# Second MLP product of a decoder block: from feature-major to token-major, each quarter as Strassen's seven half products

## The chip, the cores and the metric

The kernel runs on one core of a Trainium2 chip. The metric is the device time of one execution in microseconds (us); lower is better. Three timed runs of the kernel before gave 912.48, 912.89 and 913.3 us.

Engine names in all views: PE is the tensor engine (matmul), PEld its weight load, DVE the vector engine, ACT the scalar engine, SP the engine whose queue issues every DMA of this kernel.

## What is computed

One residual block over 512 tokens of width 1024, all in float32. The part that changes is the last one, a squared-ReLU MLP of inner width 4096:

```python
h2 = rms_norm(x) * (1.0 + scale2) + shift2
ff = jnp.square(jax.nn.relu(h2 @ w_ff1[l])) @ w_ff2[l]
x = x + gate2 * ff
```

Everything ahead of it (modulation, one input projection, a recurrent branch, a differential attention branch, their gated merge) stays as it was.

## The kernel before, in words

A float32 product runs as three passes of a faster format, float32r: every operand is split into H (rounded, by an ACT copy) and L (the rest, by a DVE subtraction), and `mm3` (L123 to L126) issues H\*H, H\*L and L\*H. Each pass is one matmul of a 128x128 stationary operand and 512 moving columns. Activations lie feature-major, 128 features by 512 tokens in a chunk, and the weights are stationary.

`load_w` brings a weight block of 128x1024 (512 KB) by DMA into one of three `w` buffers and splits it into `wh` (ACT, L118) and `wl` (DVE, L119), two buffers of each. `project` (L128) then runs 8 chunks times 3 passes = 24 matmuls into one PSUM bank.

The MLP goes in four quarters of the inner width (`qd` 0 to 3). In the first half of a quarter, the hidden half, 8 blocks of `w_ff1` are projected; each result gets ReLU (ACT, L828), is squared (DVE, L829) and split into `rh` (ACT, L833) and `rlo` (DVE, L138). In the second half 8 blocks of `w_ff2` are projected from these chunks, and DVE adds each result times gate2 into `x1` (L854). In quarter 0 two hidden blocks (`f1e`) run early, before the norm is known, and eight chunks of the modulation (`ada_chunk`, L183 on DVE, from a `w` buffer too) are computed beside the second product. The last block of all runs in two halves of the tokens (L847), each with its own output DMA.

The order of instructions on each engine is fixed when the program is built: a scheduler orders them by priority (`tc.high_priority(HP)` moves the weight splits ahead of other work), and each engine then takes its own in that order, waiting on semaphores where an operand or a buffer is not ready.

Of the kernel before, what the change touches and what calls it, by code (L numbers as in the profile page):

```python
# [44 lines left out]
DV0, DV1 = (0,), (0,)      # token blocks that the vector engine scales  # L45
# [3 lines left out]
# columns of the per-feature parameter table  # L49
# [4 lines left out]
def build(tc, out, x, xT_in, c, pos, vecs, reps, ada, w_xr, w_xr7, w_qk, w_v, w_gr, w_gm, w_lru,  # L54
# [4 lines left out]
    with ExitStack() as es:  # L59
# [21 lines left out]
        def rsqrt(dst, src, n, mul, eps, name):  # L81
            """dst = 1/sqrt(src*mul + eps), [P, n] float32, Newton from a bit-pattern seed."""
# [40 lines left out]
        def mm3(ps, lh, ll, rh, rl, first, last):  # L123
            nc.tensor.matmul(ps, lh, rh, start=first, stop=False)  # L124
            nc.tensor.matmul(ps, lh, rl, start=False, stop=False)  # L125
            nc.tensor.matmul(ps, ll, rh, start=False, stop=last)  # L126
# [35 lines left out]
        # silu(c) on every partition  # L162
# [23 lines left out]
        def ada_halves(j, k, prev=None):  # L186
            """The same in two halves of the width, from other buffers than the weights'."""
# [27 lines left out]
        # keeps the tensor engine's clock up until the first products; not read  # L215
# [17 lines left out]
        def bcast_cols(src, name, *where):  # L233
            """[P tokens, 4] -> PSUM [P, 512] with the token values on every partition."""
# [8 lines left out]
        def scale_x(j, cols, dve, p_act=None):  # L243
            """x * rs of a part of the width: blocks dve on the vector engine."""
# [14 lines left out]
        NK = 7      # blocks of the first projection that accumulate chunk by chunk  # L259
# [33 lines left out]
        rep = tmp.tile([P, 6, 64], F32, name="rep", tag="a", bufs=B_A)  # L293
# [31 lines left out]
        # sp4 = 4*softplus(-lam) = 8*s*(1 + p) + 4*max(-lam, 0)  # L325
# [14 lines left out]
        nlam = const.tile([P, 1], F32, name="nlam")   # -lambda  # L340
# [5 lines left out]
        # rope angles [P tokens, 4 blocks, 32]  # L346
# [106 lines left out]
        def lru_scan(n, a, u, prev):  # L453
            # a = exp(-8 r sp), sqrt(1 - a^2) = sqrt(tanh(4 r sp)) * (1 + a)
# [49 lines left out]
        def qk_quarter(qt):  # L504
            """q and k of two heads, token-major: rms norm, rope."""
# [28 lines left out]
        def qk_transpose(qt, rot):  # L534
            """to [2 maps x 64, tokens] (H, L), per head (q, k)"""
# [15 lines left out]
        def softmax_step(hd, q, k, i, rr):  # L551
            """e0 - lam * (s0 / s1) * e1 for one query block; 1/s0, 1/s1 go to rr."""
# [6 lines left out]
            # the two maps hold different rows of the array  # L559
# [39 lines left out]
        def head_norm(hd, po, rr):  # L599
            # o = po * r0; y = o / rms(o): one factor r0 * rsqrt(mean(po^2) r0^2 + eps)  # L600
# [18 lines left out]
        def head_out(hd, o1):  # L619
            """y^T [v features, tokens] (H, L)"""  # L620
# [46 lines left out]
        def fill():  # L667
            """The products beside the attention heads, in the order of PLAN."""
# [70 lines left out]
        # sigmoid(z) = (1 + tanh(z/2)) / 2; the halves go into gate1  # L739
# [17 lines left out]
        for n in range(KC):  # L757
# [12 lines left out]
            # x1 * (1 + scale2), before the norm  # L770
# [5 lines left out]
        shf = const.tile([P, 8, 2], F32R, name="shf")      # shift2 as (H, L)  # L776
# [10 lines left out]
        rb2 = t_("rb2s", tag="a")  # L787
# [31 lines left out]
        for qd in range(4):  # L819
            r2_ = []  # L820
            for n in range(KC):
                rl = t_(f"rl{qd}_{n}")
# [6 lines left out]
                nc.vector.tensor_tensor(rl, rl, rl, op=ALU.mult)  # L829
                i = 2 * n  # L830
                tags = [("y", B_Y)] * 2 if qd % 2 == 1 else [("q", B_Q) if i + j < 12 else ("v", B_V) for j in (0, 1)]
                rh = slot(*tags[0], f"rh{qd}_{n}", F32R)
                nc.scalar.copy(rh, rl)  # L833
                rlo = slot(*tags[1], f"rlo{qd}_{n}", F32R)
                split_l(rlo, rl, rh)
                r2_.append((rh, rlo))
            for n in range(KC):
                if qd == 3 and n == KC - 1:
                    # the last block in two halves of the tokens: a short tail
                    wh, wl = load_w(w_ff2[qd, n])  # L840
                    for hf in range(2):
                        cols = slice(hf * 256, hf * 256 + 256)
                        ps = bank(f"f2_{qd}_{n}_{hf}")[:, :256]
                        for k in range(KC):
                            c0 = slice(k * P, (k + 1) * P)
                            mm3(ps, wh[:, c0], wl[:, c0], r2_[k][0][:, cols], r2_[k][1][:, cols], k == 0, k == KC - 1)
# [76 lines left out]
```

## Time and profile before

| what | value |
|---|---|
| timed runs | 912.48, 912.89, 913.3 us |
| profiled execution, span from first to last instruction | 910.9 us |
| what lies around the span (median of the runs less the span; the page names no total of its own) | 2.0 us |
| PE, DVE, ACT busy in the span | 899.2, 572.2, 388.7 us |
| first matmul of the first second product (quarter 0) | at 602.36 us |
| one half of a quarter (192 matmuls) | 43.5 us |
| last matmul starts | at 907.46 us |

The views read are: the page (busy time by engine, granted clock in 40 slices), busy time by stretch, groups of instructions by line, and the timeline, in which a row gives start and duration in us, engine, line, operation, output<-inputs, and in brackets the idle time before it with what ended it. A PE row's duration is modelled and overlaps the next row; the distance between starts is what a matmul costs.

### The profile page before, as it was taken

Reading aid. Unit: us, or ns where it says so; the run is one execution under the profiler, and the core shown is the slowest. Engines: PE = TensorE matmul, PEld = TensorE weight load, DVE = VectorE, ACT = ScalarE, POOL = GpSimd, SP = SyncE. Lnnn points to the kernel's source line nnn. Section 1 sums busy time; section 2 is a strip of 40 time slices with the busy share of each in tenths; the row PEclk is TensorE's granted clock in tenths of the full one; section 3 lists DMA queues with packets and bytes.
Section 4 is the critical chain, followed back from the end, with each engine's and each line's share of the span. In section 5 each row is a group of like instructions: output and inputs, shape, how many; then the busy total and the mean of one; then the engine's idle time right before and its main releaser. Section 6 shows DMA issues by size and latency. Waiting matters only on the chain.

```text
span 910.9 us, 11122 instructions
## 1 busy us (share of the span) xinstructions
PE 899.2 (99%) x4204; PEld 723.0 (79%) x4204; DVE 572.2 (63%) x1080; ACT 388.7 (43%) x676; POOL 2.1 (0%) x40
## 2 busy tenths in 40 slices
PE   6999999999999999999999999999999999999998
PEld 3888887777867878777788888888888888888887
DVE  6963975697879755997758556866343344434442
ACT  6663648964454433445433333531232233213420
POOL 0000000000000000000000000000000000000000
PEclk9999999999999999999999999999999999999999
DMA  9843222122211432444445332255233222332231
GB/s 324 334 152 103 93 92 70 47 70 70 92 63 55 140 114 98 157 150 141 140 146 199 119 121 73 93 183 187 94 106 102 93 92 93 101 108 93 92 139 47
DMA packets 34473, 108.98 MB, mean 120 GB/s; under 512 B 4082, under 2 KB 4466, under 8 KB 34420
## 3 DMA queue, kind: packets, MB, share of 16 engines
q1 hardware_dynamic: 34420, 108.28, 35.0%
q8 instruction: 33, 0.54, 0.2%
q14 instruction: 20, 0.16, 0.1%
HBM read 106.17 MB, written 2.10 MB: 119 GB/s over the span
## 4 chain that ended last, share of the span: by engine, by line
PE 91%; DVE 5%; DMA 2%; ACT 1%; issue 1%; SPq 0%; ACTq 0%; DVEq 0%
PE f L124 12%; PE f L125 12%; PE f L126 12%; PE gm L125 3%; PE gm L124 3%; PE gm L126 3%; PE sc L563 3%; PE qk L126 2%; PE qk L124 2%; PE qk L125 2%; PE po L596 2%; PE v L124 2%; PE v L126 2%; PE v L125 2%; PE xr L126 2%; PE xr L124 2%
## 5 line engine op out<-in xcount | busy, mean ns | idle before, releaser
L118 ACT CAST wh<-w 128x1024 fp32r<-128x1024 f32 (+1 forms) x145 | 151.7, 1046 | 353.5 <-PE f L125 177.1
L119 DVE TENSOR_TENSOR wl<-w,wh 128x1024 fp32r<-128x1024 f32 (+1 forms) x145 | 176.3, 1216 | 124.4 <-ACT wh L118 119.8
L125 PE MATMUL f<-rlo,wh 128*128 128x512 f32 (+1 forms) x264 | 101.1, 383 | 0.0
L126 PE MATMUL f<-rh,wl 128*128 128x512 f32 (+1 forms) x264 | 101.0, 383 | 0.0
L124 PE MATMUL f<-rh,wh 128*128 128x512 f32 (+1 forms) x264 | 101.0, 383 | 0.0
L126 PE MATMUL f<-h2h,wl 128*128 128x512 f32 x240 | 93.3, 390 | 0.1
L124 PE MATMUL f<-h2h,wh 128*128 128x512 f32 x240 | 93.2, 390 | 0.0
L125 PE MATMUL f<-h2l,wh 128*128 128x512 f32 x240 | 92.7, 389 | 0.0
L854 DVE SCALAR_TENSOR_TENSOR x<-f,mod,x 128x512 f32<-128x512 f32 x31 | 23.3, 751 | 87.4 <-PE f L126 87.4
L125 PEld LDWEIGHTS f<-rlo,wh 128*128 128x128 f32 x264 | 49.6, 188 | 10.0 <-DVE rlo L138 0.4
L126 PEld LDWEIGHTS f<-rh,wl 128*128 128x128 f32 x264 | 49.6, 188 | 9.7
L124 PEld LDWEIGHTS f<-rh,wh 128*128 128x128 f32 x264 | 49.6, 188 | 9.7
L126 PEld LDWEIGHTS f<-h2h,wl 128*128 128x128 f32 x240 | 45.0, 188 | 10.0 <-DVE wl L119 0.6
L125 PEld LDWEIGHTS f<-h2l,wh 128*128 128x128 f32 x240 | 45.1, 188 | 9.4
L124 PEld LDWEIGHTS f<-h2h,wh 128*128 128x128 f32 x240 | 45.0, 188 | 9.2
L183 DVE CUSTOM_DVE_ANT_0 ada<-ada,cb,bada 128x1024 f32<-128x1024 f32 x32 | 41.0, 1282 | 17.2 <-DMA ada<-in_ada 17.1
L124 PE MATMUL gm<-hh,wh 128*128 128x512 f32 x128 | 51.5, 402 | 0.0
L126 PE MATMUL gm<-hh,wl 128*128 128x512 f32 x128 | 51.5, 402 | 0.0
L124 PE MATMUL qk<-wh,hh 128*128 128x512 f32 x128 | 51.2, 400 | 0.0
L125 PE MATMUL gm<-hl,wh 128*128 128x512 f32 x128 | 51.1, 399 | 0.0
L126 PE MATMUL qk<-wh,hl 128*128 128x512 f32 x128 | 50.7, 396 | 0.0
L125 PE MATMUL qk<-wl,hh 128*128 128x512 f32 x128 | 50.4, 393 | 0.0
(317 smaller groups left out, 1752.1 us busy)
## 6 DMA issues: line engine op xcount, KB each, us to landing
w<-in_w_ff SPq DMA_DIRECT2D x64, 512.0 KB, 3.2
ada<-in_ada SPq DMA_DIRECT2D x32, 512.0 KB, 3.3
ada<-in_ada SPq DMA_DIRECT2D x32, 256.0 KB, 5.8
w<-in_w_qk SPq DMA_DIRECT2D x16, 512.0 KB, 3.2
w<-in_w_gm SPq DMA_DIRECT2D x16, 512.0 KB, 3.3
w<-in_w_gr SPq DMA_DIRECT2D x8, 512.0 KB, 3.3
w<-in_w_v SPq DMA_DIRECT2D x8, 512.0 KB, 3.2
w<-in_w_pr SPq DMA_DIRECT2D x8, 512.0 KB, 3.2
```

The lines of the kernel that those rows point to most:

```text
L118: i_w = nc.scalar.copy(wh[:, :n], w[:, :n])
L119: nc.vector.tensor_tensor(wl[:, :n], w[:, :n], f32(wh)[:, :n], op=ALU.subtract)
L124: nc.tensor.matmul(ps, lh, rh, start=first, stop=False)
L125: nc.tensor.matmul(ps, lh, rl, start=False, stop=False)
L126: nc.tensor.matmul(ps, ll, rh, start=False, stop=last)
L183: nc.vector.tensor_tensor_reduce(w, w, cb, 1.0, bada[:, col:col + 1], op0=ALU.mult, op1=ALU.add, accum_out=mod[:, col:col + 1])
L563: nc.tensor.matmul(ps[m][:, :nn], q[lq][rows, qc], k[rk][rows, :nn], start=lq + rk == 0, stop=False)
L596: nc.tensor.matmul(po[:, i * P:n], aT[:, j * P:(j + 1) * P], v[j][:, vc * P:(vc + 1) * P], start=(j == 0), stop=(j == i))
L854: nc.vector.scalar_tensor_tensor(x1[n], ps, mcol(5, n), x1[n], op0=ALU.mult, op1=ALU.add)
```

## The change

The hidden half keeps its matmuls; its results stay unsplit in two tiles `raw` (inner chunks 0 to 3 and 4 to 7), and the square moves from DVE to ACT. The second product is turned: the activations are stationary (128 tokens by 128 inner features) and the weights move (512 output columns). A quarter is then a product of 2x2 blocks (A: token half by inner half, B: inner half by output half) and is made by seven products in place of eight, in Winograd's form, with sums of blocks made on DVE: `sums` adds blocks of weights, `sx` and the difference in `A[0][0]` are sums of activations, `split_a` and `split_b` split each operand (128x1024 elements a time, or two pieces of 512), and `add_c` gathers the results into eight token-major tiles `C`. Each product `p1`, `p5`, `p6`, `p3`, `p7`, `p2`, `p4` has 4 chunks x 2 token blocks x 3 passes = 24 matmuls into a pair of banks (X, Z or Y). At the end `finish` transposes `C` back on PE (32 transposes) and adds it into `x1`. The MLP's buffers lie where those of the mixer were (`mix_es.close()`).

```diff
-        for qd in range(4):
-            r2_ = []
             for n in range(KC):
-                rl = t_(f"rl{qd}_{n}")
+                rl = raw[n // 4][:, n % 4, :]
...
-                nc.vector.tensor_tensor(rl, rl, rl, op=ALU.mult)
...
-                rh = slot(*tags[0], f"rh{qd}_{n}", F32R)
-                nc.scalar.copy(rh, rl)
-                rlo = slot(*tags[1], f"rlo{qd}_{n}", F32R)
-                split_l(rlo, rl, rh)
-                r2_.append((rh, rlo))
+                nc.scalar.activation(rl, rl, AF.Square)
+            return raw
...
+                        b = ff.tile([P, 4, 2 * P], F32, name=f"b{qd}_{k}{c}{hf}", tag="b", bufs=8)
+                        k0 = (4 * k + 2 * hf) * P
+                        nc.sync.dma_start(b, w_ff2[qd, 4 * c:4 * c + 4, :, k0:k0 + 2 * P].rearrange("n p f -> p n f"))
...
+            def split_b(b, name, odd):
...
+                if odd:
+                    wh = wpool.tile([P, 1024], F32R, name=f"{name}h", tag="wh", bufs=2)
+                    wl = wpool.tile([P, 1024], F32R, name=f"{name}l", tag="wl", bufs=2)
+                else:
+                    wh = ff.tile([P, 1024], F32R, name=f"{name}h", tag="bh", bufs=2)
+                    wl = ff.tile([P, 1024], F32R, name=f"{name}l", tag="bl", bufs=2)
...
+            X = [bank(f"X{qd}_{t}", "sc", 2) for t in range(2)]
+            b11 = get_b(0, 0)
+            product("p1", split_a(A[0][0], "a11", 2), b11, X, True)
+            sx = ff.tile([P, 4, H2], F32, name=f"sx{qd}", tag="sx", bufs=1)
+            for i in range(2):
+                q = slice(2 * i, 2 * i + 2)
+                nc.vector.tensor_tensor(sx[:, q], A[1][0][:, q], A[1][1][:, q], op=ALU.subtract)
+            s1 = split_a(sx, "s1", 2)
+            add_c(0, 0, X, 1)
+            b12 = get_b(0, 1)
+            sums(b11, b12)
+            Z = [bank(f"Z{qd}_{t}") for t in range(2)]
+            product("p5", s1, b11, Z, True)
+            nc.vector.tensor_tensor(sx, sx, A[0][0], op=ALU.subtract)
+            s2 = split_a(sx, "s2")
+            add_c(1, 1, Z, 1)
+            b22 = get_b(1, 1)
+            sums(b11, b22)
+            product("p6", s2, b11, X, False)
...
         for qd in range(4):
-            for n in range(KC):
...
-                ps = project(w_ff2[qd, n], r2_, f"f2_{qd}_{n}")
-                if qd == 0:
+            raw = hidden(qd)
+            if qd == 0:
+                for n in range(KC):
                     ada_chunk(5, n)
-                nc.vector.scalar_tensor_tensor(x1[n], ps, mcol(5, n), x1[n], op0=ALU.mult, op1=ALU.add)
...
+            out_product(qd, raw)
```

The order of instructions shows three places. The first is DVE in quarter 0, from the split of hidden block 7 on (before). Names: `wlN` weight L parts, `rl`, `rlo` hidden results, `adaN` modulation chunks.

```order
L119 TENSOR_TENSOR wl88_5712<-w88_5709,wh88_5711 128x1024
L829 TENSOR_TENSOR rl0_5_5632<-rl0_5_5632 128x512
L138 TENSOR_TENSOR rlo0_5_5668<-rl0_5_5632,rh0_5_5666 128x512
L183 ISA ada41_5812,mod_121<-ada41_5812,cb_108,bada_117 128x1024
L183 ISA mod_121 128x1
L119 TENSOR_TENSOR wl89_5749<-w89_5746,wh89_5748 128x1024
L829 TENSOR_TENSOR rl0_6_5670<-rl0_6_5670 128x512
L138 TENSOR_TENSOR rlo0_6_5706<-rl0_6_5670,rh0_6_5704 128x512
```

The same place of DVE after the change, at the end of quarter 0's hidden half (`p5_0_1l` is the L part of product p5's second weight piece in quarter 0, `b0_...` the weights, `s1l` the L part of p5's activations):

```order
L886 TENSOR_TENSOR p5_0_1l_5815<-b0_001_5751,p5_0_1h_5814 128x1024
L188 ISA ada47_5744,mod_124<-ada47_5744,cb_111,bada_120 128x1024
L188 ISA mod_124 128x1
L919 TENSOR_TENSOR b0_001_5751<-b0_001_5751,b0_111_5851 128x1024
L886 TENSOR_TENSOR p6_0_0l_5856<-b0_000_5749,p6_0_0h_5855 128x1024
L919 TENSOR_TENSOR b0_011_5804<-b0_011_5804,b0_111_5851 128x1024
L886 TENSOR_TENSOR p6_0_1l_5860<-b0_001_5751,p6_0_1h_5859 128x1024
L927 TENSOR_TENSOR sx0_5791<-r2_0_0_5517,r2_0_1_5518 128x512
L143 TENSOR_TENSOR s1l0_5795<-sx0_5791,s1h0_5794 128x512
```

All eight modulation chunks now stand in the queue ahead of `s1l`, the last operand of p5; the ones not shown (ada40 to ada46) lie between the weight splits before these rows.

The second place is DVE in quarter 1, where the hidden half ends and the second product begins. Before (the second product's weights are one split a block, between additions into `x1`):

```order
L829 TENSOR_TENSOR rl1_7_6292<-rl1_7_6292 128x512
L138 TENSOR_TENSOR rlo1_7_6328<-rl1_7_6292,rh1_7_6326 128x512
L854 SCALAR_TENSOR_TENSOR x1_0_5020<-f2_1_0_6336,mod_121,x1_0_5020 128x512
L119 TENSOR_TENSOR wl107_6397<-w107_6394,wh107_6396 128x1024
L854 SCALAR_TENSOR_TENSOR x1_1_5060<-f2_1_1_6368,mod_121,x1_1_5060 128x512
L119 TENSOR_TENSOR wl108_6429<-w108_6426,wh108_6428 128x1024
```

After, from the fourth instruction behind the hidden half's end on (ahead of these stand `p5_1_1l`, the second piece of `sx1` and a sum of weights):

```order
L143 TENSOR_TENSOR s1l1_6367<-sx1_6363,s1h1_6366 128x512
L886 TENSOR_TENSOR p6_1_0l_6428<-b1_000_6321,p6_1_0h_6427 128x1024
L899 TENSOR_TENSOR C000_5509<-C000_5509,X1_0_6319 128x512
L899 TENSOR_TENSOR C001_5510<-C001_5510,X1_1_6320 128x512
L886 TENSOR_TENSOR p6_1_1l_6432<-b1_001_6323,p6_1_1h_6431 128x1024
L919 TENSOR_TENSOR b1_000_6321<-b1_000_6321,b1_100_6545 128x1024
L919 TENSOR_TENSOR b1_001_6323<-b1_001_6323,b1_101_6547 128x1024
L886 TENSOR_TENSOR p3_1_0l_6467<-b1_110_6421,p3_1_0h_6466 128x1024
L934 TENSOR_TENSOR sx1_6363<-sx1_6363,r2_1_0_6053 128x1024
L886 TENSOR_TENSOR p3_1_1l_6471<-b1_111_6423,p3_1_1h_6470 128x1024
L899 TENSOR_TENSOR C110_5515<-C110_5515,Z1_0_6380 128x512
L143 TENSOR_TENSOR s2l1_6416<-sx1_6363,s2h1_6415 128x1024
```

Where two instructions a block stood, fifteen now stand between the end of the hidden half and `s2l`, which p6 needs; the sums for p4 and the splits for p3, which come later on PE, are ahead of it.

The third place is PE at the start of p6 in quarter 1, after the change (before, this engine only repeats the three passes of a block):

```order
L129 MATMUL X1_0_6319<-p6_1_0h_6427,s2h1_6415 128x512
L130 MATMUL X1_0_6319<-p6_1_0l_6428,s2h1_6415 128x512
L129 MATMUL X1_1_6320<-p6_1_0h_6427,s2h1_6415 128x512
L130 MATMUL X1_1_6320<-p6_1_0l_6428,s2h1_6415 128x512
L131 MATMUL X1_0_6319<-p6_1_0h_6427,s2l1_6416 128x512
```

Four matmuls of p6 stand ahead of the first that reads `s2l`; p5 in quarter 0 has the same pattern with `s1l`.

## Rows read from the trace of the kernel before

**Rows 1.** The page: span, and granted PE clock in 40 slices.
```profile
span 910.9 us, 11122 instructions
...
PEclk9999999999999999999999999999999999999999
```

**Rows 2.** Busy time by stretch: us, PE, PEld, DVE, ACT, POOL, clock, DMA.
```profile
602.60:646.10 43.50, 43.50 (x192) 35.74 (x191) 24.29 (x30) 9.33 (x10) 0.00 (x0) 1.00 0.55 181
646.10:689.60 43.50, 43.50 (x193) 36.02 (x193) 19.62 (x23) 16.21 (x22) 0.00 (x0) 1.00 0.28 97
```

**Rows 3.** Timeline: first second product on PE; two additions a block apart on DVE.
```profile
602.36 0.39 PE L124 MATMUL f<-rh,wh 128*128 128x512 f32 x1
...
640.91 0.75 DVE L854 SCALAR_TENSOR_TENSOR x<-f,mod,x 128x512 f32<-128x512 f32 x1 [3.36 <-PE f L126]
...
646.35 0.75 DVE L854 SCALAR_TENSOR_TENSOR x<-f,mod,x 128x512 f32<-128x512 f32 x1 [3.35 <-PE f L126]
```

**Rows 4.** Groups by line, 560 to 911 us: count, busy us, mean ns, idle before.
```profile
L118 ACT CAST wh<-w 128x1024 fp32r<-128x1024 f32 x62 | 65.3, 1054 | 188.7 <-PE f L125 177.1 <-issue 6.2 <-PE shift2w L802 3.1
L828 ACT ACTIVATE rl<-f 128x512 f32<-128x512 f32 x30 | 17.6, 585 | 0.0
...
L119 DVE TENSOR_TENSOR wl<-w,wh 128x1024 fp32r<-128x1024 f32 x62 | 75.9, 1225 | 68.2 <-ACT wh L118 65.2
L829 DVE TENSOR_TENSOR rl<-rl 128x512 f32<-128x512 f32 x32 | 21.8, 685 | 0.0
L183 DVE CUSTOM_DVE_ANT_0 ada<-ada,cb,bada 128x1024 f32<-128x1024 f32 x8 | 10.3, 1284 | 5.2 <-DMA ada<-in_ada 5.2
L824 DVE TENSOR_TENSOR rl<-f1e,rb2s 128x512 f32<-128x512 f32 x2 | 1.4, 684 | 0.0
```

**Rows 5.** Timeline of DVE: starts of instructions that follow each other.
```profile
579.60 1.22 DVE L119 TENSOR_TENSOR wl<-w,wh 128x1024 fp32r<-128x1024 f32 x1 [0.99 <-ACT wh L118]
580.74 0.68 DVE L138 TENSOR_TENSOR rlo<-rl,rh 128x512 fp32r<-128x512 f32 x1
581.34 0.68 DVE L829 TENSOR_TENSOR rl<-rl 128x512 f32<-128x512 f32 x1
...
591.61 1.28 DVE L183 CUSTOM_DVE_ANT_0 ada<-ada,cb,bada 128x1024 f32<-128x1024 f32 x1 [1.26 <-DMA ada<-in_ada]
...
592.86 1.23 DVE L119 TENSOR_TENSOR wl<-w,wh 128x1024 fp32r<-128x1024 f32 x1
```

**Rows 6.** Timeline of ACT: a cast and the instruction behind it.
```profile
578.51 1.05 ACT L118 CAST wh<-w 128x1024 fp32r<-128x1024 f32 x1 [0.95 <-PE f L125]
579.47 0.62 ACT L833 CAST rh<-rl 128x512 fp32r<-128x512 f32 x1
```

**Rows 7.** Timeline: a matmul, and the cast that waited for it.
```profile
895.94 0.39 PE L125 MATMUL f<-rlo,wh 128*128 128x512 f32 x1
...
896.36 1.06 ACT L118 CAST wh<-w 128x1024 fp32r<-128x1024 f32 x1 [4.38 <-PE f L125]
```

**Rows 8.** DMA issues, 560 to 911 us: count, KB each, median us to landing.
```profile
w<-in_w_ff SPq DMA_DIRECT2D x59, 512.0 KB, 3.2
ada<-in_ada SPq DMA_DIRECT2D x8, 512.0 KB, 4.1
```

**Rows 9.** Timeline of PE: four transposes of 128x128.
```profile
418.25 0.61 PE L623 MATMUL yT<-ident,o 128*128 128x128 f32 x4
```

**Rows 10.** Timeline, the end: last matmul, last addition, its DMA issue.
```profile
907.46 0.28 PE L126 MATMUL f<-rh,wl 128*128 128x256 f32 x1
907.78 0.48 DVE L847 SCALAR_TENSOR_TENSOR x<-f,mod,x 128x256 f32<-128x256 f32 x1 [2.39 <-PE f L126]
908.29 0.33 SPq L849 DMA_DIRECT2D out_dram<-x  x1
```

**Rows 11.** Timeline of PE: full float32 matmuls (two records each), early and later.
```profile
10.58 4.21 PE L217 MATMUL warm<-x,ones 128*128 128x512 f32 x4 [4.68 <-DMA x<-in_x]
...
16.82 1.05 PE L124 MATMUL xr<-hh,wh 128*128 128x512 f32 x3
...
561.31 1.02 PE L240 MATMUL rb<-rb2d,ones 128*128 128x512 f32 x2
```

More of the change, by code (lines that the diff above doesn't have):

```diff
@@ L121, in load_w, with mm3 @@
             return wh, wl
[L123 to L126, printed above, removed]
+        def mm3(ps, lh, ll, rh, rl, first, last, more=False):
+            nc.tensor.matmul(ps, lh, rh, start=first, stop=False, skip_group_check=more)
+            nc.tensor.matmul(ps, lh, rl, start=False, stop=False, skip_group_check=more)
+            nc.tensor.matmul(ps, ll, rh, start=False, stop=last, skip_group_check=more)
         def project(src, act, name):
@@ L786, in build @@
         rb2p = bcast_cols(rs2, "rb2", "sc", 2)
-        rb2 = t_("rb2s", tag="a")
+        rb2 = t_("rb2s")
         nc.scalar.copy(rb2, rb2p)
@@ L837, in build @@
-            for n in range(KC):
-                if qd == 3 and n == KC - 1:
-                    wh, wl = load_w(w_ff2[qd, n])
-                    for hf in range(2):
[L842 to L846, printed above, removed]
-                        nc.vector.scalar_tensor_tensor(x1[n][:, cols], ps, mcol(5, n), x1[n][:, cols],
-                                                       op0=ALU.mult, op1=ALU.add)
-                        nc.sync.dma_start(out[n][:, cols], x1[n][:, cols])
-                    continue
-                ps = project(w_ff2[qd, n], r2_, f"f2_{qd}_{n}")
-                if qd == 0:
+                nc.scalar.activation(rl, rl, AF.Square)
@@ new lines, in hidden, with out_product, get_b, split_a @@
+            return raw
+        def out_product(qd, raw):
+            A = [[raw[k][:, :, r * H2:(r + 1) * H2] for k in range(2)] for r in range(2)]
+            B = {}
+            def get_b(k, c):
+                if (k, c) not in B:
+                    B[k, c] = []
+                    for hf in range(2):
+                        b = ff.tile([P, 4, 2 * P], F32, name=f"b{qd}_{k}{c}{hf}", tag="b", bufs=8)
+                        k0 = (4 * k + 2 * hf) * P
+                        nc.sync.dma_start(b, w_ff2[qd, 4 * c:4 * c + 4, :, k0:k0 + 2 * P].rearrange("n p f -> p n f"))
+                        B[k, c].append(b)
+                return B[k, c]
+            def split_a(src, name, parts=1):
+                ah = ff.tile([P, 4, H2], F32R, name=f"{name}h{qd}", tag="ah", bufs=3)
+                al = ff.tile([P, 4, H2], F32R, name=f"{name}l{qd}", tag="al", bufs=3)
+                for i in range(parts):
+                    q = slice(i * 4 // parts, (i + 1) * 4 // parts)
+                    nc.scalar.copy(ah[:, q], src[:, q])
+                    split_l(al[:, q], src[:, q], ah[:, q])
+                return ah, al
+            def split_b(b, name, odd):
+                v = b.rearrange("p n (k f) -> p k n f", f=P)
+                if odd:
[4 more added lines that the diff above has]
+                    wl = ff.tile([P, 1024], F32R, name=f"{name}l", tag="bl", bufs=2)
+                v4 = lambda t: t.rearrange("p (k n f) -> p k n f", k=2, f=P)
+                with tc.high_priority(HP):
+                    nc.scalar.copy(v4(wh), v)
+                    nc.vector.tensor_tensor(v4(wl), v, f32(v4(wh)), op=ALU.subtract)
+                flat = lambda t: t.rearrange("p (k f) -> p k f", k=2)
+                return flat(wh), flat(wl)
+            seen = set()
+            def add_c(r, c, ps, sign):
+                for t in range(2):
+                    dst = C[r][c][t]
+                    if qd == 0 and (r, c, t) not in seen:
+                        seen.add((r, c, t))
+                        nc.scalar.activation(dst, ps[t], AF.Copy, scale=float(sign))
+                    else:
+                        nc.vector.tensor_tensor(dst, dst, ps[t], op=ALU.add if sign > 0 else ALU.subtract)
+            def product(name, a, bs, ps, first, by_block=False, done=None):
+                fs = [split_b(b, f"{name}_{qd}_{i}", i) for i, b in enumerate(bs)]
+                order = [(hf, t) for hf in range(2) for t in range(2)]
+                if by_block:
+                    order = [(hf, t) for t in range(2) for hf in range(2)]
+                for hf, t in order:
+                    for kk in range(2):
+                        k = 2 * hf + kk
+                        ts = slice(t * P, (t + 1) * P)
+                        mm3(ps[t], a[0][:, k, ts], a[1][:, k, ts], fs[hf][0][:, kk], fs[hf][1][:, kk],
+                            first and k == 0, k == 3, not first)
+                    if done is not None and hf == 1:
+                        done(t)
+            def sums(dsts, srcs):
+                with tc.high_priority(HP):
+                    for d, s_ in zip(dsts, srcs):
+                        nc.vector.tensor_tensor(d, d, s_, op=ALU.add)
+            X = [bank(f"X{qd}_{t}", "sc", 2) for t in range(2)]
[17 more added lines that the diff above has]
+            product("p6", s2, b11, X, False)
+            nc.vector.tensor_tensor(sx, sx, A[0][1], op=ALU.add)
+            s4 = split_a(sx, "s4")
+            add_c(0, 1, X, -1)
+            product("p3", s4, b22, Z, False)
+            nc.vector.tensor_tensor(A[0][0], A[0][0], A[1][0], op=ALU.subtract)
+            s3 = split_a(A[0][0], "s3")
+            add_c(0, 1, Z, 1)
+            sums(b12, b22)
+            product("p7", s3, b12, X, False)
+            a12 = split_a(A[0][1], "a12")
+            add_c(1, 1, X, -1)
+            b21 = get_b(1, 0)
+            Y = [bank(f"Y{qd}_{t}") for t in range(2)]
+            product("p2", a12, b21, Y, True)
+            a22 = split_a(A[1][1], "a22")
+            sums(b11, b21)
+            add_c(0, 0, Y, 1)
+            if qd < 3:
+                product("p4", a22, b11, X, False)
+                add_c(1, 0, X, 1)
+                return
+            for n in range(4, KC):
+                finish(n, 0, 4)
+            def done(t):
+                nc.vector.tensor_tensor(C[1][0][t], C[1][0][t], X[t], op=ALU.add)
+                if t == 0:
+                    for n in range(4):
+                        finish(n, 0, 3)
+                else:
+                    for n in range(4):
+                        finish(n, 3, 4)
+            product("p4", a22, b11, X, False, by_block=True, done=done)
@@ new lines, in build, with finish @@
+        n_fin = [0]
+        def finish(n, t0, t1):
+            pt = bank(f"cT{n}_{t0}", *(("tp", 1), ("o", 1))[n_fin[0] % 2])
+            n_fin[0] += 1
+            for t in range(t0, t1):
+                nc.tensor.transpose(pt[:, t * P:(t + 1) * P], C[t // 2][n // 4][t % 2][:, n % 4 * P:(n % 4 + 1) * P],
+                                    ident)
+            cols = slice(t0 * P, t1 * P)
+            nc.vector.scalar_tensor_tensor(x1[n][:, cols], pt[:, cols], mcol(5, n), x1[n][:, cols],
+                                           op0=ALU.mult, op1=ALU.add)
+            nc.sync.dma_start(out[n][:, cols], x1[n][:, cols])
```

23 lines of the change are left out of this document (15 added, 8 removed).

## The prediction

> **What bounds the kernel now.** I read the page first: the span of the profiled execution is 910.9 us, and the granted clock is full in all 40 slices [rows 1]. The timed runs have a median of 912.89, so 2.0 us lie around the span, and I make every sum against the span and add 2.0. Then the busy time by stretch, for the part that changes: in the second product of quarter 0 and in the hidden half behind it PE has a matmul in all of the 43.5 us, while DVE is busy 24.29 and 19.62 and ACT 9.33 and 16.21 [rows 2]. So PE alone sets the time there, and the additions on DVE, which follow each other a block apart, wait for it each time: 5.44 us for 24 matmuls, or 0.2267 each [rows 3]. Both other engines have room, but DVE is half used already, and the change puts its new work there. The question is whether DVE stays ahead of PE.
>
> Everything before the first matmul of the first second product, at T0 = 602.36 [rows 3], keeps its order, so I count from T0.
>
> **What goes.** Seven products of 24 matmuls take the place of eight blocks of 24, four times: 96 matmuls less, at 0.2267 that is 21.8 us of PE. A second product without a wait would take 168 x 0.2267 = 38.1 us. The moving operand keeps 512 columns, so I take the same price for a matmul; the hidden half keeps its 192.
>
> **What DVE gets.** In one second product: 14 splits of weights, 7 of activations, 8 sums of weights and 4 of activations (all counted in pieces of 1024 elements), and 14 additions into C of 512. Their prices from the nearest rows: instructions that stand ready in DVE's queue follow each other 1.14 us apart at 1024 elements and 0.60 at 512 [rows 5], though each is busy 1.225 and 0.685 [rows 4]. C's addition has an operand in PSUM; so has the row of 0.684, no dearer than the one without [rows 4]. Sum: 33 x 1.14 + 14 x 0.60 = 46 us, against 38.1 of PE. Part of this runs ahead, in the hidden half, where DVE has some 24 us free and loses the squares (ACT takes them: 8 more activations of 0.585 beside 16.21 busy in 43.5, which costs nothing [rows 2, 4]). So DVE can hold the mean, but not every place.
>
> [...]
>
> **Quarters 1 to 3.** The second weight piece of p5 is cast by ACT when the last pass of the hidden half that reads the old buffer is done: that matmul starts 0.45 before the half's end, its release comes 0.42 after its start [rows 7], so the cast runs from about 0 to 1.05 [rows 4]. Behind it stand fifteen DVE instructions up to the end of `s2l`: nine of 1.14, five of 0.60, and the last in full, 1.22. That is 10.26 + 3.0 + 1.22 = 14.5, so `s2l` is ready 15.5 after the half's end. PE wants it for p6's fifth matmul, at 48 x 0.2267 + 4 x 0.2267 = 11.8. PE waits 3.7, most of it (2.8) at p6's first matmul, for the cast `s2h`, which needs `sx` from the same queue (its start 11.4, 1.22, then 1.05 on ACT), the rest at the fifth for `s2l`. The same walk for the rest gives `s4l` at 19.5 where PE wants it at 20.1 and `s3l` at 24.3 for 25.5, and the splits of the next hidden block at 39.6 for 41.8: no other wait, but DVE is only 0.6 to 2 us ahead. A second product takes 38.1 + 3.7 = 41.8 against 43.5: 3 x -1.7 = **-5.1**.
>
> The bounds of this: two lengths give the price of a link per element, (1.14 - 0.60)/512, and with no fixed part the chain is 0.06 x 14 = 0.8 shorter a quarter; with full busy times it is 1.1 longer. That makes 3 x (-2.5 to -0.6), with all else as above.
>
> **Quarter 0.** The eight modulation chunks, which lay between the additions, now all stand ahead of `s1l` on DVE. Each is a transfer of 512 KB into one of three `w` buffers, 4.1 us from issue to landing [rows 8], and each chunk of DVE, 1.25 to the next start [rows 5], frees a buffer for a later one. Walked from the last splits of the hidden half, the fourth chunk can start 3.4 before T0. From there five chunks at 1.25, seven pieces of 1.14, one of 0.60 and the last in full (0.69) are 15.5: `s1l` is ready at T0 + 12.2, where p5 wants it at 5.44 + 0.91 = 6.35. The wait is 5.85, and p5 ends at 16.7. From `s1l` on the queue holds five of 1.14 and a 0.60 up to `s2l`, held up a little by three of ACT's casts, which follow each other 0.96 apart [rows 6]: `s2l` is ready at T0 + 20.8, where p6 wants it at 16.7 + 0.9 = 17.6: another 3.2. So 38.1 + 5.85 + 3.2 = 47.1 against 43.5: **+3.6**. If the chunks land in 3.2, as the weights do [rows 8], it is 2 less; the smaller pieces in which the new weights come (1 KB rows, for which no row stands) may make it 3 to 6 more (rival 3).
>
> **The end.** Of 32 transposes 28 stand on PE inside quarter 3's p4: at 0.113 apart (four in 0.61, the last not followed [rows 9]) **+3.2**, at most 0.15 each, 4.3. Behind the last product now come the last addition into C (0.68 with 0.42 for the release), four transposes in two pairs (0.6 with release each), the small additions into `x1` (0.48 [rows 10]) and the DMA issue: 5.15 to the end of the span where 3.3 stood behind the last matmul's end (907.6 to 910.9): **+1.9**. The last block's two half passes no longer fall in halves: **-0.6**.
>
> Sum: -5.1 + 3.6 + 3.2 + 1.9 - 0.6 = +3.0, on a span of 910.9 with 2.0 around it: **916**. Its own range is 911 to 920 (bounds of the links, -2.5 and +3.3; transposes +1.1; landing -2).
>
> **The rivals.** 0.2% of the time, 1.8 us, is about what a measurement of this kernel can tell from no change.
>
> 1. *Faster: quarter 0 doesn't wait for the modulation.* Place: p5 of quarter 0. If the chunks' transfers start early enough that all eight are done before T0, `s1l` comes in time and the whole 9.0 of waits goes: 907. For it: the 3.2 us that transfers of this size take elsewhere [rows 8], and DVE's free time before T0. Against: three buffers, which the hidden half's weights use as well. It decides when the fourth chunk starts 4.8 us earlier than I walked it (from there the change is faster by over 1.8).
> 2. *The clock falls in the waits.* [...] PE's new waits are 2.8 to 5.9 long in a stretch where it had none. [...] Against: the page shows no fall behind the shorter waits of the kernel before [rows 1]. [...]
> 3. *The new weights' transfers are slow.* They come as 128 x 4 pieces of 1 KB and stand in the same queue as the modulation in quarter 0. If they take the queue longer, all of quarter 0's chain moves: 919 to 922. In quarters 1 to 3 eight buffers cover it. Against: the share of DMA is 0.55 at most [rows 2].
> 4. *DVE's links cost their busy time.* 0.08 more for each of 14 links in three quarters and some 18 in quarter 0: 921.
>
> That the change would not do what it says is out: the order of PE counts 168 matmuls where 192 stood, and all fifteen DVE rows are there.
>
> **How the numbers follow.** My walk 0.50, rival 1 0.22, rival 2 0.13, rival 3 0.11, rival 4 0.04. The predicted time is the walk's, 916. Faster by over 0.2%: most of rival 1, 0.22 with the walk's low end; within 0.2% (911.1 to 914.7): the walk's lower part and a partial rival 1, 0.19; slower: 0.59. For 8 in 10 the range goes down into rival 1 and up past one or two falls of the clock: 906 to 926.
>
> **What would show it.** PE idle ahead of p6 in quarters 1 to 3, about 2.8 for `s2h` and 0.9 for `s2l`, and in quarter 0 about 5.9 ahead of or in p5 for `s1h` and `s1l`; DVE without idle time between those ends; hidden halves still 43.5; transposes 0.113 apart; matmuls at 0.2267 behind each wait (at twice that, rival 2 holds); 5.1 from the last product matmul to the end. Waits at p3, p7, p2 or p4, or a DVE that idles for ACT's casts, would make the walk wrong.

## The result and the profile after

The changed kernel takes 921.64 us (median of four runs, 920.7 to 923.3) against 912.68 of the kernel before in the same series: 1.0102 times as long, 95% interval 1.009 to 1.0115, or 9 us more. The forecast was 916 with a range of 906 to 926: the sign and the range held, but the change costs three times what the sum gave. The profiled execution read below is one of the two longer ones of the four (922.55 and 923.3, at a mean granted clock of 0.987; the other two, 920.73 and 920.7, have 0.991).

The page of the profiled execution: the span, PE's busy share and granted clock in 40 slices.

```profile
span 920.5 us, 11108 instructions
...
PE   7999999999999999999999999989998999899987
...
PEclk9999999999999999999999999989999999999999
```

Before, PE had work all the time and the clock was full in all slices [rows 1]. Now PE has four dents, one in the second product of each quarter, and the end; in one of them (it is quarter 0's) even the slice's clock is down.

Busy time by stretch, to be read beside [rows 2]: the second products of quarters 0, 1 and 2, and quarter 3's up to its last product matmul; us, then PE, PEld, DVE, ACT, POOL, granted clock, DMA share and GB/s.

```profile
602.15:651.00 48.85, 43.20 (x169) 34.35 (x168) 40.91 (x43) 25.07 (x29) 0.00 (x0) 0.90 0.41 132
...
694.50:737.90 43.40, 40.07 (x169) 32.42 (x168) 39.36 (x42) 21.35 (x22) 0.00 (x0) 0.96 0.33 106
...
781.40:824.10 42.70, 39.96 (x170) 32.41 (x170) 39.35 (x42) 21.36 (x22) 0.00 (x0) 0.96 0.34 107
...
867.60:914.70 47.10, 43.76 (x197) 34.88 (x195) 39.64 (x45) 18.13 (x19) 0.00 (x0) 0.96 0.09 33
```

The 168 matmuls that took the place of 192 are there (quarter 3's stretch also has 28 transposes), but they take 48.85, 43.4 and 42.7 us where 192 took 43.5, and PE is not busy for 2.7 to 5.7 us in each. What the counts don't explain is the clock column: 0.90 and 0.96 where it was 1.00.

Where PE waits, in quarter 1 (its second product begins at 694.52). Timeline of PE: the last matmul of p5, the first matmuls of p6, and where its pace returns.

```profile
705.18 0.39 PE L131 MATMUL Z<-p_1h,s1l 128*128 128x512 f32 x1
708.31 0.50 PE L129 MATMUL X<-p_0h,s2h 128*128 128x512 f32 x1 [2.74 <-ACT s2h L870]
708.64 0.40 PE L130 MATMUL X<-p_0l,s2h 128*128 128x512 f32 x1
...
709.11 0.40 PE L130 MATMUL X<-p_0l,s2h 128*128 128x512 f32 x1
710.10 0.79 PE L131 MATMUL X<-p_0h,s2l 128*128 128x512 f32 x1 [0.59 <-DVE s2l L143]
710.69 0.63 PE L129 MATMUL X<-p_0h,s2h 128*128 128x512 f32 x1
711.12 0.63 PE L130 MATMUL X<-p_0l,s2h 128*128 128x512 f32 x1
...
713.18 0.39 PE L131 MATMUL X<-p_0h,s2l 128*128 128x512 f32 x1
713.41 0.40 PE L129 MATMUL X<-p_1h,s2h 128*128 128x512 f32 x1
```

And DVE in the same stretch, from the start of the chain of fifteen to its end.

```profile
695.59 1.22 DVE L886 TENSOR_TENSOR p_1l<-b,p_1h 128x1024 fp32r<-128x1024 f32 x1 [1.70 <-ACT p_1h L885]
...
702.55 2.35 DVE L919 TENSOR_TENSOR b<-b,b 128x1024 f32<-128x1024 f32 x2
704.83 1.22 DVE L886 TENSOR_TENSOR p_0l<-b,p_0h 128x1024 fp32r<-128x1024 f32 x1
705.96 1.22 DVE L934 TENSOR_TENSOR sx<-sx,r 128x1024 f32<-128x1024 f32 x1
...
708.83 1.22 DVE L143 TENSOR_TENSOR s2l<-sx,s2h 128x1024 fp32r<-128x1024 f32 x1
```

The chain ends at 710.05, 15.53 after the second product's start, where 15.5 was forecast. PE stands idle for 2.74 ahead of `s2h` and for 0.59 ahead of `s2l`. The forecast counted from start to start: 3.13 and 0.99, less the 0.23 of a matmul, are 2.90 and 0.76, 3.7 in all, where 2.8 and 0.9 were forecast. So the walked queue holds. What was not in the sum is what follows: from 710.69 a matmul starts 0.43 after the one before it, not 0.2267, until about 713, and then the old pace is back. The granted clock in that stretch, and in the same stretch of quarter 0's p5:

```profile
710.10:712.80 2.70, 2.70 (x6) 2.15 (x7) 2.70 (x3) 0.99 (x1) 0.00 (x0) 0.50 0.43 146
...
611.90:617.50 5.60, 5.58 (x13) 4.41 (x14) 4.66 (x5) 1.06 (x2) 0.00 (x0) 0.50 0.02 3
```

At a granted clock of 0.50 a matmul starts 0.427 after the one before it, where 0.2267 goes with 1.00. This is the forecast's rival 2, the clock that falls in the waits, five times in this execution: in quarter 0 at p5 and p6, in each other quarter at p6.

Quarter 0, PE at p5, and DVE at the modulation's fourth chunk and at `s1l`.

```profile
608.27 0.39 PE L130 MATMUL Z<-p_0l,s1h 128*128 128x512 f32 x1
611.92 0.79 PE L131 MATMUL Z<-p_0h,s1l 128*128 128x512 f32 x1 [3.27 <-DVE s1l L143]
612.51 0.63 PE L129 MATMUL Z<-p_0h,s1h 128*128 128x512 f32 x1
...
617.82 0.39 PE L129 MATMUL Z<-p_1h,s1h 128*128 128x512 f32 x1
```

```profile
596.52 1.28 DVE L188 CUSTOM_DVE_ANT_0 ada<-ada,cb,bada 128x1024 f32<-128x1024 f32 x1 [0.36 <-DMA ada<-in_ada]
...
611.19 0.68 DVE L143 TENSOR_TENSOR s1l<-sx,s1h 128x512 fp32r<-128x512 f32 x1
```

The fourth chunk starts 5.6 ahead of the second product's start, not 3.4, so PE stands idle for 3.27 (3.42 from start to start), where 5.85 was forecast. The fall behind it lasts until 617.6.

The end: the last product matmul, DVE's last addition into C, the last transposes (line 983), the last addition into x1.

```profile
914.49 0.40 PE L131 MATMUL X<-p_1h,a22l 128*128 128x512 f32 x1
914.92 0.69 DVE L966 TENSOR_TENSOR C<-C,X 128x512 f32<-128x512 f32 x1 [0.78 <-PE X L131]
915.67 0.20 PEld L983 LDWEIGHTS cT<-ident,C 128*128 128x128 f32 x2 [1.22 <-DVE C L966]
...
916.81 0.61 DVE L986 SCALAR_TENSOR_TENSOR x<-cT,mod,x 128x128 f32<-128x128 f32 x2 [0.16 <-PE cT L983]
```

From the last product matmul's end (914.72) to the end of the span are 5.8 us, where 3.3 stood before [rows 10].

### The profile page after: what moved, and what is told of

It is laid out like the page before. It is cut to its first block, busy times and chain, and to the rows that moved or that the text cites. A ratio compares the mean times of both kernels' runs of the same rounds, so it can differ in the third digit from the quotient of the medians.

```text
span 920.5 us, 11108 instructions
## 1 busy us (share of the span) xinstructions
PE 892.4 (97%) x4116; PEld 712.2 (77%) x4116; DVE 656.9 (71%) x1155; ACT 447.5 (49%) x744; POOL 2.1 (0%) x40
## 4 chain that ended last, share of the span: by engine, by line
PE 82%; DVE 11%; DMA 2%; ACT 2%; issue 1%; SPq 0%; DVEq 0%; ACTq 0%
PE f L130 5%; PE f L129 5%; PE f L131 5%; PE gm L129 3%; PE gm L130 3%; PE gm L131 3%; PE X L131 3%; PE sc L568 3%; PE X L129 2%; PE qk L131 2%; PE X L130 2%; PE qk L130 2%; PE qk L129 2%; PE po L601 2%; DVE b L919 2%; PE v L129 2%
## 5 line engine op out<-in xcount | busy, mean ns | idle before, releaser
L122 ACT CAST wh<-w 128x1024 fp32r<-128x1024 f32 (+1 forms) x113 | 118.0, 1044 | 243.3 <-PE f L130 60.5
L123 DVE TENSOR_TENSOR wl<-w,wh 128x1024 fp32r<-128x1024 f32 (+1 forms) x113 | 137.0, 1213 | 124.4 <-ACT wh L122 122.8
L188 DVE CUSTOM_DVE_ANT_0 ada<-ada,cb,bada 128x1024 f32<-128x1024 f32 x32 | 40.9, 1281 | 16.6 <-DMA ada<-in_ada 16.6
L885 ACT CAST p_1h<-b 128x1024 fp32r<-128x1024 f32 x28 | 29.5, 1052 | 36.8 <-PE f L130 18.4
L576 ACT ACTIVATE e<-sc,nm 128x128 f32<-128x128 f32 (+3 forms) x64 | 33.5, 527 | 26.7 <-DVE nm L574 26.4
L886 DVE TENSOR_TENSOR p_1l<-b,p_1h 128x1024 fp32r<-128x1024 f32 x28 | 34.2, 1220 | 16.5 <-ACT p_1h L885 16.5
L885 ACT CAST p_0h<-b 128x1024 fp32r<-128x1024 f32 x28 | 29.5, 1053 | 27.7 <-PE X L131 11.5
L886 DVE TENSOR_TENSOR p_0l<-b,p_0h 128x1024 fp32r<-128x1024 f32 x28 | 34.1, 1220 | 8.1 <-ACT p_0h L885 8.1
L919 DVE TENSOR_TENSOR b<-b,b 128x1024 f32<-128x1024 f32 x32 | 38.8, 1219 | 0.2
L574 DVE TENSOR_REDUCE nm<-sc 128x1 f32<-128x128 f32 (+3 forms) x64 | 29.7, 483 | 2.8 <-PE sc L571 2.7
```

Source lines behind the costliest of these rows:

```text
L122: i_w = nc.scalar.copy(wh[:, :n], w[:, :n])
L123: nc.vector.tensor_tensor(wl[:, :n], w[:, :n], f32(wh)[:, :n], op=ALU.subtract)
L188: nc.vector.tensor_tensor_reduce(w, w, cb, 1.0, bada[:, col:col + 1], op0=ALU.mult, op1=ALU.add, accum_out=mod[:, col:col + 1])
L574: nc.vector.tensor_reduce(nm, ps[m][:, :n], axis=AX.X, op=ALU.max, negate=True)
L576: nc.scalar.activation(e[:, :n], ps[m][:, :n], AF.Exp, bias=nm, accum_out=sums[:, m:m + 1])
L885: nc.scalar.copy(v4(wh), v)
```

## The experiments

The theory to test: the seven products cost what the rows before say; the time is lost where PE waits for DVE's queue (the order in it, not its sum) and again behind each such wait, where PE runs at the lower clock (0.50 in the stretches above). Rivals: DVE has too much work in any order; the slow matmuls are slow for another reason. Each run is compared with the kernel before, run beside it on the same chip (912.0 to 912.7); differences to the changed kernel are taken against its 921.64.

**e1: the modulation chunks later.** In program order they stand behind quarter 0's second product, ahead of the next hidden half.

```diff
+            out_product(qd, raw)
             if qd == 0:
                 for n in range(KC):
                     ada_chunk(5, n)
-            out_product(qd, raw)
```

> Only the eight modulation chunks move: in the program they are now written behind quarter 0's second product, so six of them leave DVE's queue ahead of s1l. Theory (PE loses the waits for DVE's queue, and behind each long wait some 1.6 to 3 us more at the lower clock): quarter 0's second product falls from 48.9 us to about 39, its waits to under 1 us and no clock fall there; quarters 1 to 3 as they were; about 911.5 us in all, 10 below the changed kernel's 921.6. Rival (DVE has too much work, whatever its order): the chunks are late later, the next hidden half or quarter 1 becomes longer by about as much, and the time stays within 2 us of 921.6.

Measured: 913.56, 1.0013 times the kernel before (1.0003 to 1.0023), 8.1 below the changed kernel. Busy time by stretch, quarter 0's second product and the hidden half behind it:

```profile
602.00:641.90 39.90, 39.04 (x170) 31.38 (x169) 39.61 (x42) 24.48 (x29) 0.00 (x0) 1.00 0.53 168
641.90:685.40 43.50, 43.50 (x193) 36.02 (x192) 16.75 (x16) 18.67 (x26) 0.00 (x0) 1.00 0.25 85
```

39.9 in place of 48.85, the granted clock is 1.00, and nothing comes back in the hidden half. PE's two waits that are left (0.27 and 0.60, at p6) leave the clock alone. Three chunks still run ahead of the first piece of `s1l`, three run between its pieces, and two come 20 us later. So 9 us of this quarter were the chunks' place in DVE's queue: 4.8 of them PE's idle time (5.65 before, 0.87 now), the rest mostly the lower clock behind it.

**e2: only s2 first.** What an engineer would try first on seeing PE wait for `s2h` and `s2l`.

```diff
-            nc.vector.tensor_tensor(sx, sx, A[0][0], op=ALU.subtract)
-            s2 = split_a(sx, "s2")
+            with tc.high_priority(HP):
+                nc.vector.tensor_tensor(sx, sx, A[0][0], op=ALU.subtract)
+                s2 = split_a(sx, "s2")
```

> Only the priority of p6's activation sum and split (sx for s2, s2h, s2l) is raised, to that of the weight splits. Theory with the queue walked: p6 no longer waits, but s4's chain now stands behind two additions, two sums and p7's splits, so p3 waits about 2.9 + 0.9 in quarters 1 to 3, and the clock falls there in place of p6: 919 to 924, no gain. Rival (the place of s2 in the queue is all that costs): the waits and the clock falls of three quarters go, 3 x 5.3: about 906.

Measured: 920.95, 1.0088 (1.0073 to 1.0103), 0.7 below the changed kernel and within its spread. Timeline of PE in quarter 1, at the start of p3:

```profile
711.00 0.50 PE L129 MATMUL Z<-p_0h,s4h 128*128 128x512 f32 x1 [3.15 <-ACT s4h L870]
...
712.79 0.53 PE L131 MATMUL Z<-p_0h,s4l 128*128 128x512 f32 x1 [0.58 <-DVE s4l L143]
713.13 0.63 PE L129 MATMUL Z<-p_0h,s4h 128*128 128x512 f32 x1
```

In quarters 1 to 3 the wait has moved from p6 to p3 with its size (3.15 for 2.74) and with the clock's fall behind it (matmuls 0.43 apart from 713.13 on); p6 itself runs through. Quarters 1 and 2 take 44.0 and 43.1, 0.6 and 0.5 more than in the changed kernel. Quarter 0 did gain: its second product takes 44.6 in place of 48.85, since the wait of 2.15 for `s2l` and the fall behind it are gone. (This run's second product of quarter 0 begins 1.1 later than in the changed kernel, 603.27 for 602.15, for a reason ahead of the edit.)

**e3: PE busy in the wait.** In quarters 1 to 3 two full float32 matmuls that nothing reads stand between p5 and p6 (`p5`, `p6` hold the matmuls of the products; `after` sets the order on one engine).

```diff
+            if qd > 0:
+                kp = bank(f"keep{qd}", "o", 1)
+                ks = [nc.tensor.matmul(kp, ones, x1[0], start=True, stop=True) for i in range(2)]
+                for k0 in ks:
+                    after(k0, p5[-1][1])
+                    for m in p6:
+                        after(m[0], k0)
```

> In quarters 1 to 3 two full float32 matmuls, whose result nothing reads, stand on PE between p5 and p6 and fill 2.0 of the 2.7 us that PE waits there; nothing else moves. Theory (the slow matmuls behind the wait are the clock, which fell because PE stood still): no matmul of p6 at 0.43 in quarters 1 to 3, the waits end where they ended, and each quarter is 1.6 to 1.9 shorter: about 916.3. Rival (they are slow because their operands are just being written, or by DVE and ACT beside them): p6 as slow as before, 921.6 or up to 1 us more.

Measured: 918.08, 1.0058 (1.0043 to 1.0073), 3.6 below the changed kernel, 5.3 expected. Timeline of PE in quarter 1:

```profile
705.35 1.88 PE L944 MATMUL keep<-x,ones 128*128 128x512 f32 x4
708.24 0.50 PE L129 MATMUL X<-p_0h,s2h 128*128 128x512 f32 x1 [1.02 <-ACT s2h L870]
...
710.04 0.50 PE L131 MATMUL X<-p_0h,s2l 128*128 128x512 f32 x1 [0.61 <-DVE s2l L143]
710.37 0.39 PE L129 MATMUL X<-p_0h,s2h 128*128 128x512 f32 x1
710.60 0.40 PE L130 MATMUL X<-p_0l,s2h 128*128 128x512 f32 x1
```

`s2h` and `s2l` come when they came, but p6's matmuls stand 0.23 apart in these three quarters, the first behind a wait 0.33 to 0.36, and the mean granted clock of the run is 0.995 where the changed kernel had 0.987. The edit leaves DVE's and ACT's work beside them as it was; so the slow matmuls were the clock's, and it fell where PE stood still for 2.74, not where it had work for 1.88 of that time. The gain is smaller than p6's 1.6 to 1.9 each because the fall also covers something: in quarter 2 p6 is slow from its first matmul on, so `s2l` is ready when the fifth comes, and the second product is only 0.6 longer than with the clock up (42.62 to 42.01; in quarter 1 43.40 to 42.02, in quarter 3 up to p4 38.17 to 36.57).

**e8: the same with one matmul**, `range(1)` in the edit above, so that it fills half as much.

> As the run in which two full float32 matmuls fill the wait ahead of p6 in quarters 1 to 3, but one: it fills 1.0 of the 2.7 us, so 1.7 are left. Theory (the clock falls when PE stands still long enough): either no matmul of p6 at 0.43, and the time as with two, 918; or a fall as without any, 921.6. Rival (what slows p6 is DVE and ACT writing beside it, and the two matmuls only shifted it): part of the slow matmuls stays in each quarter, about 920.

Measured: 920.51, 1.0097 (1.0069 to 1.0124), between the two in the median, but with runs from 918.86 to 924.92. In the profiled run the wait at p6 is 1.88 (1.87 in quarter 3) and then 0.61; in quarter 1 the clock fell behind it (matmuls 0.43 apart), in quarters 2 and 3 it did not (0.23). Timeline of PE, quarter 1:

```profile
709.12 0.50 PE L129 MATMUL X<-p_0h,s2h 128*128 128x512 f32 x1 [1.88 <-ACT s2h L870]
...
710.91 0.80 PE L131 MATMUL X<-p_0h,s2l 128*128 128x512 f32 x1 [0.61 <-DVE s2l L143]
711.50 0.63 PE L129 MATMUL X<-p_0h,s2h 128*128 128x512 f32 x1
```

The same in quarter 2:

```profile
795.98 0.50 PE L129 MATMUL X<-p_0h,s2h 128*128 128x512 f32 x1 [1.88 <-ACT s2h L870]
...
797.77 0.50 PE L131 MATMUL X<-p_0h,s2l 128*128 128x512 f32 x1 [0.61 <-DVE s2l L143]
798.10 0.40 PE L129 MATMUL X<-p_0h,s2h 128*128 128x512 f32 x1
```

Equal waits, to the hundredth, with and without a fall: the length of a wait alone did not decide it here. What else does is open.

**e4: the sums for p4 late.** Two sums that PE wants some 20 us later stood ahead of `s2l` by their priority.

```diff
-            def sums(dsts, srcs):
-                with tc.high_priority(HP):
+            def sums(dsts, srcs, hp=HP):
+                with tc.high_priority(hp):
...
-            sums(b11, b21)
+            sums(b11, b21, 1)
```

> Only the two sums of weights for p4 lose their priority, so they no longer stand ahead of s2l. Theory: in quarters 1 to 3 the waits at p6 shrink to 0.3 and at p3 there is one of about 0.9, too short for the clock to fall: each of these quarters is 2.1 (waits) + 1.8 (clock) shorter, about 910 us. Rival 1 (slow matmuls are not the clock's): only the 2.1 each, 915. Rival 2 (DVE has too much work): the waits come back at p4 or in the next hidden half and the time stays at 921.

Measured: 912.84, 0.9999 (0.999 to 1.0009), 8.8 below the changed kernel. The waits in quarter 1:

```profile
707.40 0.50 PE L131 MATMUL X<-p_0h,s2l 128*128 128x512 f32 x1 [0.76 <-DVE s2l L143]
...
713.73 0.50 PE L131 MATMUL Z<-p_0h,s4l 128*128 128x512 f32 x1 [0.58 <-DVE s4l L143]
```

Two short waits at p6 and p3 without a fall (matmuls 0.23 apart behind both), none at p4 or in the hidden half. It is not DVE's amount of work. PE's order moved a little too: four matmuls of p2 now stand among those of p7, and neither waits. The forecast of 910 was 2.8 low: quarters 1 and 2 and quarter 3 up to p4 gained 3.35, 2.55 and 3.55 where 3.9 each was expected; three falls cost 3.6 (e3), not 5.4, and the waits that are left are 0.76 and 0.58, where 0.3 and 0.9 were walked.

**e5: both edits**, of e1 and e4, together.

> The two edits that each worked by themselves, together: the modulation chunks written behind quarter 0's second product, and the two sums for p4 without priority. Theory: the gains add, since they are waits at different places: 921.6 - 8.1 - 8.8 = 904.7, between 903 and 906.5; no wait of PE over 1 us and no matmul at 0.43. Rival (DVE has too much work once PE is faster): waits over 1 us in the hidden halves or at p4, 908 to 913.

Measured: 904.54, 0.991 (0.9897 to 0.9924). The gains add to 0.2 us: two separate causes at two places. One part of the forecast did not hold: in quarter 0 PE waits 0.57 and then 1.13 at p6 (expected: none over 1 us), without a fall of the clock (matmuls 0.23 apart behind both), and that second product takes 40.7.

**e6: the queue by due time.** e4's edit; the sums of activations and the splits of them 40 ahead in place of none; one modulation chunk behind each weight split of quarter 1's hidden half.

```diff
+                if qd == 1:
+                    ada_chunk(5, n, last_wl[0])
...
-                    nc.scalar.copy(ah[:, q], src[:, q])
-                    split_l(al[:, q], src[:, q], ah[:, q])
+                    with tc.high_priority(40):
+                        nc.scalar.copy(ah[:, q], src[:, q])
+                        split_l(al[:, q], src[:, q], ah[:, q])
...
-            nc.vector.tensor_tensor(sx, sx, A[0][0], op=ALU.subtract)
+            with tc.high_priority(40):
+                nc.vector.tensor_tensor(sx, sx, A[0][0], op=ALU.subtract)
...
-            sums(b11, b21)
+            sums(b11, b21, 1)
...
-            if qd == 0:
-                for n in range(KC):
-                    ada_chunk(5, n)
```

> DVE's queue put into the order in which PE needs the results: sums for p4 without priority; activation sums and splits 40 ahead; one modulation chunk behind each weight split of quarter 1's hidden half. Theory: every product takes 5.44 and each second product of quarters 0 to 2 takes 38.1 to 38.3; against the changed kernel that is 10.7 in quarter 0 and 15.2 in the others, so 895.7, at most 898. Rival (the order can't do it, since DVE is ahead of PE by too little): waits of 1 to 3 us at p3, p7 or in quarter 1's hidden half with the chunks, 900 to 905.

Measured: 897.34, 0.9833 (0.9819 to 0.9846): 15.3 faster than the kernel before, 24.3 faster than the changed kernel. Busy time by stretch, the second product of quarter 0, the hidden half with the chunks, and quarter 1's second product:

```profile
602.00:640.30 38.30, 38.30 (x171) 31.71 (x169) 35.56 (x36) 24.82 (x29) 0.00 (x0) 1.00 0.38 118
640.30:683.80 43.50, 43.50 (x193) 36.04 (x192) 25.65 (x31) 18.68 (x27) 0.00 (x0) 1.00 0.57 187
683.80:722.00 38.20, 38.09 (x168) 31.19 (x167) 36.66 (x40) 19.98 (x21) 0.00 (x0) 1.00 0.33 107
```

The last stretch ends ahead of its product's end. Timeline of PE: the first matmuls of p4 in quarter 1, and the first of the hidden half behind it.

```profile
716.46 0.61 PE L130 MATMUL X<-p_0h,a22h 128*128 128x512 f32 x2
...
722.34 0.39 PE L130 MATMUL f<-h2h,wh 128*128 128x512 f32 x1
```

p4 takes 5.88 there, 0.44 over its 5.44, and 5.84 in quarter 2. So the second product of quarter 0 takes 38.1 and has no wait, those of quarters 1 and 2 take 38.5 (expected: 38.1 to 38.3), and DVE, with 36.7 us of busy time in the 38.2 shown, keeps up. Fewer matmuls are worth what was counted: 21.8 us less, of which 3.5 goes to transposes on PE, 2.5 to the longer end and 0.8 to the short waits at p4, and 0.6 more that the kernel before lost, half of it in quarter 0's second product (43.8 for 43.5) and half in the last block's two half passes; that makes 15.6, and 15.3 was measured. Against e5 it is 7.2; the run changes the place of the chunks and the priority of the activations together, and what each is worth was not run by itself.

**e7: no transposes.** From e6; x1 gets a piece of C that is not turned back.

```diff
-            for t in range(t0, t1):
-                nc.tensor.transpose(pt[:, t * P:(t + 1) * P], C[t // 2][n // 4][t % 2][:, n % 4 * P:(n % 4 + 1) * P],
-                                    ident)
+            pt = C[t0 // 2][n // 4][t0 % 2]
```

> The kernel in the order of due times, with the 32 transposes of the end left out: x1 gets a part of C as it lies, so the output is not the block's. What is missing from the time is the price of turning C back. Theory (28 transposes stand between matmuls of the last p4 and cost 0.125 each, the last four and their releases lengthen the end by 0.8 to 1.6): 897.3 - 3.5 - 1.2 = 892.6, between 891.5 and 893.5. Rival (the transposes fill gaps in which PE would wait for DVE or for a bank): under 1 us, 896.5.

Measured: 896.1, 0.9821 (0.9804 to 0.9837), 1.2 below e6, with intervals that overlap; 4.7 was expected. In the profiled run the MLP begins 1.7 later than in e6 (603.96 for 602.22), for a reason ahead of the edit (in the ten profiled runs it begins between 602.1 and 604.0), so the end is compared from there: 291.1 to 293.0, or 1.9 less. Timelines of its end, PE's last product matmul and DVE's work:

```profile
887.87 0.39 PE L132 MATMUL X<-p_1h,a22l 128*128 128x512 f32 x1
```

```profile
887.18 0.68 DVE L975 TENSOR_TENSOR C<-C,X 128x512 f32<-128x512 f32 x1
887.78 2.20 DVE L991 SCALAR_TENSOR_TENSOR x<-C,mod,x 128x384 f32<-128x384 f32 x4
889.90 0.68 DVE L975 TENSOR_TENSOR C<-C,X 128x512 f32<-128x512 f32 x1
```

PE gains: p4 takes 5.9, not 8.9. But the last addition into C, which could start at about 888.3, starts at 889.90, behind additions into x1 that are still in DVE's queue, and 7.0 us follow the last matmul in place of 5.8. The transposes mostly stand in time in which the end would wait for DVE anyway: the expectation was wrong, its rival the nearer one.

## Why the prediction came out as it did

**Right:** the sign, and how: too few matmuls saved to pay for DVE's queue in its order. The prices of DVE's links (1.14 and 0.60), by which `s2l` would be 15.5 late, gave 15.53; rival 4, in which each link costs its full busy time, is out (it would have given 16.6). The hidden halves stay at 43.5, no other product waits, the 28 transposes make p4 8.96 long where 8.64 was forecast, and rival 3 did not come about: the chunks of the modulation came earlier than walked, not later. But what it feared was hardly put to the test: between the issues of the first and the last chunk (582.95 to 600.3) only one block of the new weights is issued (583.34), the others before 575.3 or from 618.07 on, and no run shows the 3 to 6 us put down for it.

**Wrong, the step that failed:** the sum took 0.2267 for every matmul, behind the waits too, and put the clock's fall at 0.13 as rival 2. In the profiled run it fell behind all five long waits (2.15 to 3.27). The terms, from the profiled span (920.5, forecast 913.9): quarter 0 is +5.3 against the kernel before, where +3.6 stood, with 2.9 less waiting than forecast (6.1 in all from start to start, since the chunks came 2.2 earlier) and 4.6 of slow matmuls and restarts that were not in it; quarters 1 and 2 are -0.1 and -0.9 where -1.7 stood, quarter 3 up to p4 is 1.8 over its forecast; p4's transposes +0.3, the end +0.65. Nearly all of the 6.6 is behind the waits. In all, some 9.7 us of slow matmuls and restarts were not in the sum (4.6, 1.6, 1.6 and 1.9 in the four quarters), and 3.7 us less waiting than walked (2.9 in quarter 0, 0.8 in quarter 2) hid part of them: that the time lies well inside the range, and not at 925, is luck. e3 shows the clock by itself for quarters 1 to 3 (3.6 us: 1.4, 0.6 and 1.6); for quarter 0 it is read from the trace (5.6 us at a clock of 0.50 behind p5's wait), and e1 took it away together with its wait.

**Rival 2** (the clock falls in the waits) happened. The range goes up past one or two falls; no run shows the price of a fall that this is counted with. What the runs show: a fall costs 0.6 to 1.6 net in quarters 1 to 3 (e3); in the trace it lasts 3.1 to 3.6 us there and in quarter 2 covers the wait that would follow. In quarter 0, read from the trace, it costs some 2.8 at p5 and 1.9 at p6. So five falls gave 921.6, with quarter 0's wait shorter than walked. The argument against the rival, that no fall shows behind the waits of the kernel before, was empty: behind the first 18 us no wait of PE there is longer than 0.6, and the MLP has none at all.

In quarter 2, 2.74 of standing still is followed by matmuls 0.43 apart at a granted clock of 0.50. It does not go so behind every wait: behind three alike (1.87 to 1.88) in e8 the clock fell once, and behind those of 0.3 to 1.1 us that e1 left in quarter 0, e4 in quarters 1 to 3 and e5 in quarters 0 and 1 it never did.

**Rival 1** (quarter 0 doesn't wait for the modulation) did not happen; the fourth chunk came 2.2 earlier than walked, not 4.8. Taking chunks out of the queue (e1) made that second product 9 shorter, the 9.0 that the rival named, but that is luck: the rival counted waits alone (5.85 and 3.2), and of the 9 that went only 4.8 was idle time.

## What to carry to other kernels

When a change takes work from a saturated engine and gives it to a half idle one, walk the second engine's queue instruction by instruction: here its load was 39 us in 43, but the order alone made the difference between 1% slower and 1.7% faster: 17 us of it the place of two sums wanted some 20 us later and of the chunks wanted at the very end (e5), 7 the rest of e6. A priority raised for one late operand moves the wait to the next one (e2); give the queue the order of due times instead. And a wait of TensorE was dearer here than it was long: in the MLP of these runs matmuls stood 0.43 apart in place of 0.2267 behind every wait of 2.1 to 3.9 us that the timelines of the changed kernel and of e1 to e4 show, behind one of three of 1.9 (e8), and behind none of those of 1.13 or less that had no longer one just ahead (e1, e3, e4, e5). The forecast priced its waits at their length alone, and some 9.7 us behind them were not in its sum.

## What was not expected of the hardware

The clock did not always fall at the same place: in quarter 1 four matmuls stood 0.23 to 0.33 apart behind the wait of 2.74 (708.31 to 709.11) and those from 710.69 on 0.43, in quarter 2 the second followed the first by 0.59 and the others by 0.43. Two equal waits (1.88 and 0.61) in one execution (e8) had a fall behind one and none behind the other. The blocks of new weights, in pieces of 1 KB, landed 3.5 us after their issue in the median, where the blocks before took 3.2; whether they would delay the modulation's chunks (4.0, and 4.1 before) stays open, since the two hardly met.
